# Issuing the first 1 MB load of a matmul kernel as two transfers, of 16 and of 112 partitions

## The chip, the cores and the metric

The kernel runs on one core of one Trainium2 chip. The metric is the device time of one execution in microseconds (us). Every run quoted is fast: none is over 1.5% above the fastest of the same kernel. Differences here are below 1.3%, so every comparison is made with runs of the kernel before taken on the same chip in the same rounds.

The span of a profile (first to last instruction) is about 1.8 us shorter than the device time of the same run: 209.0 us against 210.74 us for the kernel before.

## The reference

```python
batch, m, k, n = 16, 512, 1024, 768          # x: 16 x 512 x 1024, weight: 1024 x 768, float32
def reference(x, weight, bias, residual):
    return (np.matmul(x, weight) + bias + residual).astype(np.float32)
```

Read as 2-D, x has 8192 rows, which are 64 tiles of 128. The kernel reads x (33.6 MB), the residual (25.2 MB) and the weights (3.1 MB), and writes 25.2 MB: 87 MB through the DMA engines.

## The kernel before

Each tile of x is cast to bf16 (`cast`), transposed on TensorE (`transp`), multiplied by the weights into PSUM, the memory that TensorE writes (`mms`), and given bias and residual (`finish`, `pool_add`). Loads go to SBUF, the on-chip memory of 128 rows, called partitions. All transfers except the bias row are issued by SP, in this order:

```python
x_d = x2d.rearrange("(S p j) k -> S p j k", p=P, j=J)      # P = 128 partitions, J = 8 tiles a group

def load_x(S, j0=0, j1=J):
    if S < n_s:
        if j0 == 0:
            x_sb[S] = ring(sb, "x_tile", S, X_BUFS, [P, J, K], FP32)
        K_(nc.sync.dma_start(out=x_sb[S][:, j0:j1, :], in_=x_d[S, :, j0:j1, :]))
...
load_x(0, 0, 2)          # the first load: two tiles, 8 KB a partition, 1 MB
load_x(0, 2, 3)
load_w(0); load_w(1); load_w(2); load_w(3)      # 768 KB each
load_x(0, 3, 4)
load_x(0, 4, 6)
load_x(0, 6, 8)
load_res(0, 0, 4)
load_x(1, 0, 4)
...
keep_warm(12)            # 12 matmuls on zeros, until the first tile is there
cast(0, "dve")
cast(1)
transp(0)
transp(1)
keep_warm(3)
...                      # tile 2, bias, casts of the weights; then the main matmuls
```

## Time and profile before

| what | kernel before | where it is read |
|---|---|---|
| device time, first three runs | 210.83 us (210.65 to 210.95) | times |
| TensorE (PE) busy | 200.4 us of 209.0 | page, part 1 |
| DMA | 98 to 100% busy, about 430 GB/s in the middle | stages |
| first two tiles landed | 5.40 us | start of the casts |
| first main matmul | 9.54 us | timeline |
| last eviction ends, span ends | 203.5 us, 209.0 us | timeline, page |

From the page of the kernel before: the busy times, the row of DMA busy tenths in 40 slices of the span, the bytes, and the chain that ended last.

```profile
PE 200.4 (96%) x1274; PEld 130.6 (63%) x1299; DVE 105.0 (50%) x139; ACT 67.6 (32%) x68; POOL 115.5 (55%) x71
...
DMA  6999999999999999999999999999999999999994
...
DMA packets 5632, 87.23 MB, mean 417 GB/s; under 512 B 625, under 2 KB 753, under 8 KB 1906
...
PE 96%; issue 1%; DVE 1%
```

Two resources look full: PE at 96%, and the DMA row, nearly all nines. The next view shows stages (start and end in us, length, busy us of each engine with instruction counts, granted TensorE clock, DMA share, GB/s).

```profile
20.00:60.00 40.00, 39.69 (x259) 26.37 (x264) 20.82 (x27) 15.19 (x17) 26.78 (x15) 1.00 1.01 428
...
204.00:209.00 5.00, 0.00 (x0) 0.00 (x0) 0.00 (x0) 0.00 (x0) 0.00 (x0) 0.87 0.40 156
```

In the middle both are full. In the last 5 us no compute engine does anything, while the DMA engines still move 156 GB/s on average. The last pieces of the chain of waits show that it stops before that (start, length, what):

```profile
199.15 3.91 PE po L104 x24
203.06 0.02 issue
203.08 0.42 DVE ro L131
```

The chain ends at 203.5 us, and the span at 209.0: the last 5.5 us, the draining of the stores, are in no line of it.

The start, from the timeline (start, busy us, engine, line, operation, count, in brackets the idle time before it and what ended it):

```profile
0.74 0.85 SPq L66 DMA_DIRECT2D x_tile<-in_x_dram  x2
1.19 5.26 PE L170 MATMUL po<-warm 128*128 128x512 bf16 x12 [1.19 <-DVE warm L156]
5.40 0.69 DVE L87 CAST xb<-x_tile 128x1024 bf16<-128x1024 f32 x1 [4.13 <-DMA x_tile<-in_x_dram]
6.28 1.04 PE L95 MATMUL pt<-ident,xb 128*128 128x128 f32 x8
7.16 0.81 PE L170 MATMUL po<-warm 128*128 128x512 bf16 x3
8.54 0.83 ACT L176 CAST w_sb<-ro 128x768 bf16<-128x768 f32 x1 [0.84 <-DMA ro<-in_weight_dram]
9.54 7.31 PE L104 MATMUL po<-w_sb,xt 128*128 128x512 bf16 x43
```

SP issues the first load at 0.74 us; the casts start when it has landed, at 5.40; the first weight slice lands at 8.54.

The DMA engines in the first 8 us, in 40 slices of 0.2 us (busy tenths, then GB/s):

```profile
DMA  0000000087945699897997959999999999999899
GB/s 0 0 0 0 0 0 0 0 164 164 328 123 164 287 492 451 369 492 328 492 410 328 573 205 389 384 430 451 410 492 389 430 430 492 399 399 461 369 430 461
```

Nothing moves before about 1.7 us, and the rate is low for the first microsecond.

### The profile page before, as it was taken

The page shows a single profiled execution, that of the slowest core. Times are in us where ns is not written, and L with a number is a line of the kernel's source. Part 1 is how long each engine was busy: PE and PEld are TensorE (multiplying, and loading weights), DVE is VectorE, ACT ScalarE, POOL GpSimd, SP SyncE. Part 2 cuts the span into 40 slices and gives each one's busy share as a digit, 9 for nine tenths or more (in the row PEclk, how much of TensorE's full clock was granted, in tenths as well). Part 3 has the DMA queues.
Part 4 walks back from the last instruction along what each step waited for, and adds up shares of the span by engine and source line. Part 5 has one row for each costly group of instructions (what it writes and reads, how often), then busy time and mean ns, then how long its engine had stood idle before and what let it go on. Part 6 is the DMA issues. An engine that isn't in the chain of part 4 may idle for free.

```text
span 209.0 us, 3151 instructions
## 1 busy us (share of the span) xinstructions
PE 200.4 (96%) x1274; PEld 130.6 (63%) x1299; DVE 105.0 (50%) x139; ACT 67.6 (32%) x68; POOL 115.5 (55%) x71
## 2 busy tenths in 40 slices
PE   7999999999999999999999999999999999999980
PEld 2566666666666666666666666666666666666650
DVE  0737465445445544554554455455445544545550
ACT  2544315511723062422443054230724233430000
POOL 2000197819965565999189802994069910799000
PEclk9999999999999999999999999999999999999998
DMA  6999999999999999999999999999999999999994
GB/s 239 427 421 431 436 413 440 442 405 436 423 470 422 419 428 398 459 420 436 433 400 472 416 427 447 412 439 412 437 445 414 445 419 427 442 419 428 426 404 168
DMA packets 5632, 87.23 MB, mean 417 GB/s; under 512 B 625, under 2 KB 753, under 8 KB 1906
## 3 DMA queue, kind: packets, MB, share of 16 engines
q1 hardware_dynamic: 5616, 87.03, 97.9%
q8 instruction: 10, 0.16, 0.3%
q14 instruction: 4, 0.03, 0.0%
q10 hardware_dynamic: 2, 0.00, 0.0%
HBM read 61.87 MB, written 25.17 MB: 416 GB/s over the span
## 4 chain that ended last, share of the span: by engine, by line
PE 96%; issue 1%; DVE 1%
PE po L104 79%; PE pt L95 13%; PE po L170 3%; PE po L190 1%; DVE xt L99 0%; DVE ro L131 0%; DVE warm L156 0%
## 5 line engine op out<-in xcount | busy, mean ns | idle before, releaser
L104 PE MATMUL po<-w_sb,xt 128*128 128x512 bf16 (+1 forms) x999 | 175.4, 324 | 1.4
L104 PEld LDWEIGHTS <-xt 128*128 128x128 bf16 x1024 | 100.1, 98 | 59.5 <-DVE xt L99 0.5
L87 ACT CAST xb<-x_tile 128x1024 bf16<-128x1024 f32 x62 | 62.8, 1044 | 114.5 <-DMA x_tile<-in_x_dram 56.9
L121 POOL TENSOR_TENSOR ro<-ro,bias_sb 128x768 f32<-128x768 f32 x40 | 71.2, 1816 | 36.2 <-DMA ro<-in_residual_dram 26.2
L99 DVE COPY xt<-pt 128x512 f32<-128x512 f32 x64 | 44.2, 691 | 86.7 <-PE pt L95 86.5
L121 POOL TENSOR_TENSOR ro<-ro,tmp 128x768 f32<-128x768 f32 x24 | 43.1, 1814 | 41.0 <-DMA ro<-in_residual_dram 30.2
L131 DVE TENSOR_TENSOR ro<-po,ro 128x768 f32<-128x768 f32 (+2 forms) x41 | 38.0, 930 | 2.9 <-PE po L104 2.8
L95 PE MATMUL pt<-ident,xb 128*128 128x128 f32 x256 | 38.2, 273 | 0.0
L95 PEld LDWEIGHTS pt<-ident,xb 128*128 128x128 f32 x256 | 29.8, 141 | 8.1 <-issue 0.6
L129 DVE TENSOR_TENSOR tmp<-po,bias_sb 128x768 f32<-128x768 f32 x24 | 22.8, 949 | 0.6 <-POOL ro L121 0.5
L170 PE MATMUL po<-warm 128*128 128x512 bf16 x15 | 6.1, 579 | 1.2 <-DVE warm L156 1.2
L176 ACT CAST w_sb<-ro 128x768 bf16<-128x768 f32 x4 | 3.3, 832 | 4.0 <-DMA ro<-in_weight_dram 4.0
L170 PEld LDWEIGHTS <-warm 128*128 128x128 bf16 x15 | 1.9, 135 | 4.1 <-issue 2.8
L87 DVE CAST xb<-x_tile 128x1024 bf16<-128x1024 f32 x2 | 1.4, 696 | 4.8 <-DMA x_tile<-in_x_dram 4.8
L178 DVE CAST w_sb<-ro 128x768 bf16<-128x768 f32 x4 | 2.2, 555 | 2.5 <-DMA ro<-in_weight_dram 2.5
L161 ACT ACT_TABLE_LOAD x1 | 1.3, 1283 | 2.0 <-POOL ident masks.py:199 2.0
L190 PE MATMUL po<-tmp 128*128 128x512 f32 (+1 forms) x4 | 1.5, 486 | 0.0
L198 DVE COPY bias_sb<-po 128x768 f32<-128x768 f32 x1 | 1.0, 958 | 0.1
L190 PEld LDWEIGHTS po<-tmp 128*128 128x128 f32 x4 | 0.7, 190 | 0.5 <-issue 0.5
L135 POOL MEMSET tmp<- 128x768 f32 x1 | 0.7, 737 | 0.3 <-POOLq L268 0.3
L156 DVE MEMSET warm<- 128x256 uint32 x1 | 0.3, 272 | 0.9 <-PEq L268 0.9
masks.py:199 POOL TENSOR_SCALAR_AFFINE_SELECT ident<-ident 128x128 f32<-128x128 f32 x1 | 0.3, 292 | 0.1
(8 smaller groups left out, 1.0 us busy)
## 6 DMA issues: line engine op xcount, KB each, us to landing
ro<-in_residual_dram SPq DMA_DIRECT2D x7, 3072.0 KB, 18.1
out_dram<-ro SPq DMA_DIRECT2D x7, 3072.0 KB, 23.9
x_tile<-in_x_dram SPq DMA_DIRECT2D x5, 4096.0 KB, 30.8
x_tile<-in_x_dram SPq DMA_DIRECT2D x4, 2048.0 KB, 27.6
x_tile<-in_x_dram SPq DMA_DIRECT2D x3, 1024.0 KB, 8.6
ro<-in_weight_dram SPq DMA_DIRECT2D x4, 768.0 KB, 9.0
ro<-in_residual_dram SPq DMA_DIRECT2D x2, 1536.0 KB, 21.1
out_dram<-ro SPq DMA_DIRECT2D x1, 1536.0 KB, 11.9
```

The lines of the kernel that those rows point to most:

```text
L87: K_(copy(out=xb[t], in_=x_sb[t // J][:, t % J, :]))
L95: K_(nc.tensor.transpose(out=pt[:, c, :], in_=pairs[:, c * P:(c + 1) * P], identity=ident))
L99: K_(nc.vector.tensor_copy(out=xt[t], in_=pt))
L104: K_(nc.tensor.matmul(po[t][:, n0:n0 + nl], lhsT=both[:, e, :], rhs=w_sb[:, c, e, n0:n0 + nl], start=(i == 0), stop=(i == len(steps) - 1),))
L121: K_(nc.gpsimd.tensor_add(out=r, in0=r, in1=tmp[t] if t < EARLY else bias_sb))
L129: K_(nc.vector.tensor_add(out=tmp[t], in0=p, in1=bias_sb))
L131: K_(nc.vector.tensor_add(out=row(t, n0, nl), in0=p, in1=row(t, n0, nl)))
L161: K_(nc.scalar.copy(out=warm_a, in_=warm_a))
L170: K_(nc.tensor.matmul(warm_ps[:, 0:512], lhsT=warm[:, 0:P], rhs=warm, start=True, stop=True))
L176: K_(nc.scalar.copy(out=w_sb[:, c, e, :], in_=w_st[:, c, e, :]))
L178: K_(nc.vector.tensor_copy(out=w_sb[:, c, e, :], in_=w_st[:, c, e, :]))
L190: K_(nc.tensor.matmul(bias_ps[:, n0:n0 + nl], lhsT=ones, rhs=bias_row[:, n0:n0 + nl], start=True, stop=True,))
```

## The change

The intent appears to be that a small first transfer gets all DMA engines going sooner. The two transfers together move the same 1 MB into the same places.

```diff
-    def load_x(S, j0=0, j1=J):
+    def load_x(S, j0=0, j1=J, p0=0, p1=P):
         if S < n_s:
-            if j0 == 0:
+            if j0 == 0 and p0 == 0:
                 x_sb[S] = ring(sb, "x_tile", S, X_BUFS, [P, J, K], FP32)
-            K_(nc.sync.dma_start(out=x_sb[S][:, j0:j1, :], in_=x_d[S, :, j0:j1, :]))
+            K_(nc.sync.dma_start(
+                out=x_sb[S][p0:p1, j0:j1, :], in_=x_d[S, p0:p1, j0:j1, :]
+            ))
...
-    load_x(0, 0, 2)
+    load_x(0, 0, 2, 0, 16)
+    load_x(0, 0, 2, 16, P)
```

## The prediction

> **What bounds the kernel now.** TensorE. The page gives PE 200.4 us busy of 209.0 (96%), and the chain that ended last is 96% PE; in the stage view PE is busy 39.7 of 40 us in the middle. The DMA engines are close behind (98-100% busy, 417 GB/s). Since PE hardly pauses after 9.5 us (longest wait 0.5 us, for DVE), a delay of the first main matmul moves the end by the same amount.
>
> **What the change does.** One 1 MB load (128 partitions x 8 KB) becomes 128 KB (partitions 0-15) plus 896 KB (16-127). Bytes, compute and the other engines' order stay. SP has 39 rows instead of 38, and its later waits on "eight DMAs ago" move by one place: the load of tile 3 now waits for the bias load, perhaps 2 us past its 3.7 us issue, but its bytes are queued behind 3 MB of weights anyway.
> - Added on SP: one issue, about 0.43 us (two take 0.85 us). Issues run ahead of the data, so it is free, except that the second transfer's descriptors come 0.43 us after the first's.
> - The intent must be an earlier start. In the DMA view of the first 4 us, the issue is at 0.74 us, first packets at 1.7, full rate (430 GB/s) from about 2.75; only about 210 KB move between 1.7 and 2.7 us. An earlier start could win some 0.3 us at most.
> - Against it: the Trainium skill, page "SBUF — State Buffer", section "Door 1: The DMA port swizzle", puts partitions 0-15 on 4 of 16 SBUF ports and gives 104 GB/s measured there. By that page 128 KB takes (estimate) 1.26 us, which holds each of the 16 engines on its single 8 KB row; before, a first packet takes 0.3-1.0 us (mean about 0.65), a later one 0.31. Then 7 rows per engine follow, 2.2 us, on partition groups not aligned with ports. No run here has shown the port effect yet.
> Net estimate: 1.26 - 0.65 = +0.6 us, less a possible 0.1-0.2 us earlier start: both tiles land at about 5.8 us instead of 5.4.
>
> **How much is critical.** Casts start on landing (5.40 us), the first transposes at 6.2 us. Warm-up weight loads are 0.43 us apart and the transposes' come 0.63 us after the last of them, so they already wait for the cast. Tile 2 (landing 6.65 us, transposes 7.75), bias matmuls (8.24), first weight slice (landing 8.5, first main matmul 9.54) are in the same DMA stream, so all move by the stream's delay. From then on PE and stream move together. About 0.3-0.4 us reaches the end.
>
> **Prediction.** 211.15 us, range 210.6 to 211.7. Faster by over 2%: 0.5%; within 2%: 99%; slower: 0.5%. Direction: slower by 0.1-0.6 us 60%, no visible change 25%, faster by 0.1-0.4 us 15%.
>
> **What the profile would show.**
> - Right: first packets still at 1.6-1.7 us; from 1.8 to 2.9 us a rate near 100-150 GB/s; first tiles landing at 5.6-6.1 us, tile 2 and the first weight slice 0.2-0.6 us later, first main matmul at 9.8-10.0 us, PE busy unchanged, total later by the same.
> - Wrong: first packets at 1.3-1.5 us, first tiles before 5.4 us, first main matmul before 9.5 us.
>
> **What would make it wrong.** (1) Buffering hides the port conflict and the smaller transfer starts sooner: up to 0.4 us faster. (2) The 112 partitions spread unevenly, slowing more than estimated. (3) The wait near 18 us absorbs the delay: no change.

## The result, and the profile after

The changed kernel takes 212.25 us (median of 6, 212.13 to 212.57), the kernel before 210.85 us (median of 6, 210.58 to 211.35) on the same chip. The ratio is 1.0067, with a 95% interval of 1.0053 to 1.0081. Here and below a ratio is the mean time of one kernel's fast runs over that of the other's fast runs of the same rounds, so it is not quite the ratio of the medians. The change costs 0.67%, about 1.4 us: inside the 2% band, but above the predicted 211.15 us and outside the range of 210.6 to 211.7.

The page of the changed kernel, the lines that answer to those of before:

```profile
PE 201.7 (96%) x1274; PEld 131.8 (63%) x1299; DVE 104.9 (50%) x139; ACT 68.3 (32%) x68; POOL 115.7 (55%) x71
...
DMA  6999999999999999999999999999999999999984
...
PE 93%; DMA 3%; DVE 1%; issue 1%; SPq 0%; DVEq 0%
```

The averages hardly move. The chain gained a DMA piece at its start. The timeline of the start shows more:

```profile
0.74 1.32 SPq L66 DMA_DIRECT2D x_tile<-in_x_dram  x3
7.41 0.69 DVE L89 CAST xb<-x_tile 128x1024 bf16<-128x1024 f32 x1 [6.13 <-DMA x_tile<-in_x_dram]
8.25 1.68 PE L97 MATMUL pt<-ident,xb 128*128 128x128 f32 x8 [2.37 <-DVE xb L89]
9.72 1.49 PE L173 MATMUL po<-warm 128*128 128x512 bf16 x3
10.41 0.83 ACT L179 CAST w_sb<-ro 128x768 bf16<-128x768 f32 x1 [0.83 <-DMA ro<-in_weight_dram]
13.20 7.31 PE L106 MATMUL po<-w_sb,xt 128*128 128x512 bf16 x43
```

Three things happened.

- The first two tiles land at 7.39 us instead of 5.40, 2.0 us late.
- The whole DMA stream behind them is late: the first weight slice lands at 10.41 instead of 8.54, 1.9 us late.
- TensorE, idle for 2.4 us, comes back slow: the eight transposes take 1.68 us instead of 1.04, the three warm-up matmuls 1.49 instead of 0.81. The first main matmul is 3.66 us late.

The Trainium skill, page "TensorE: Matmul & The Clock Gate", section "Part 1: The HAM clock gate", says that the array runs at half speed until about 3.4 us of sustained work. This trace agrees: after the pause the same instructions take 1.6 to 1.8 times as long, with a mean granted clock of 0.64 from 8 to 10 us, 0.51 from 10 to 12, and 1.00 from 12 on. In the traces the granted clock fell to 0.5 after every early pause of TensorE of 2.0 to 3.6 us (the change, e6, e7, e8, e10, e12), and not after those of 0.5 to 1.1 us (e3, e4, e11).

The DMA engines in the first 8 us, after:

```profile
DMA  0000000059399207497989769898889996899999
GB/s 0 0 0 0 0 0 0 0 123 369 164 328 205 41 0 246 164 492 287 410 246 410 179 164 369 246 410 246 225 225 266 205 266 184 328 451 369 492 461 420
```

The first packets do not come earlier (1.75 us in both traces), and from 3 to 6.6 us the engines are busy but move only 281 GB/s on average, against 414 before. The packet records, of which the views print only sums, give the same in another form: of the 128 packets of 8 KB that make up the load, 19 took over 350 ns before and 108 do now; packets 17 to 128, all of the 112-partition transfer, take 490 ns on average instead of 319. The first 16, the small transfer, take 455 ns, less than the 654 ns of the first 16 before, and have all ended at 2.40 us. So by these records it is the packets of the large transfer that are slow, not those of the small one. Whether the first 14 of the large one (756 to 1146 ns) wait for the small one cannot be told. The stage from 3 to 6 us, after the change:

```profile
3.00:6.00 3.00, 2.88 (x9) 0.88 (x7) 0.00 (x0) 0.50 (x2) 0.00 (x0) 1.00 0.96 288
```

At the end, the last pieces of the chain after the change:

```profile
202.81 3.92 PE po L106 x24
206.72 0.02 issue
206.75 0.42 DVE ro L133
```

TensorE is still 3.66 us late (206.72 against 203.06), but the span grew by only 1.8 us in these two profiles and the time by 1.4 us. A delay of TensorE by 3.66 us therefore did not reach the end as such. Either some of it vanished in slack and the rest counts, or only the DMA stream counts, whose delay (1.5 to 1.9 us) is about the size of the loss. To have one figure for the stream I use the time at which its first 40 MB had ended, from the packet records: 96.78 us before, 98.41 after, 1.63 us later.

### The profile page after: what moved, and what is told of

Read it like the earlier page. It is cut to its first block, busy times and chain, and to the rows that moved or that the text cites. A ratio compares the mean times of both kernels' runs of the same rounds, so it can differ in the third digit from the quotient of the medians.

```text
span 210.8 us, 3154 instructions
## 1 busy us (share of the span) xinstructions
PE 201.7 (96%) x1274; PEld 131.8 (63%) x1299; DVE 104.9 (50%) x139; ACT 68.3 (32%) x68; POOL 115.7 (55%) x71
## 4 chain that ended last, share of the span: by engine, by line
PE 93%; DMA 3%; DVE 1%; issue 1%; SPq 0%; DVEq 0%
PE po L106 78%; PE pt L97 14%; DMA x_tile<-in_x_dram 3%; PE po L193 1%; PE po L173 1%; DVE xb L89 0%; DVE xt L101 0%; DVE ro L133 0%; SPq L66 0%; DVEq L89 0%
## 5 line engine op out<-in xcount | busy, mean ns | idle before, releaser
L89 ACT CAST xb<-x_tile 128x1024 bf16<-128x1024 f32 x62 | 63.5, 1045 | 117.5 <-PE pt L97 67.1
L97 PE MATMUL pt<-ident,xb 128*128 128x128 f32 x256 | 39.3, 278 | 2.4 <-DVE xb L89 2.4
L97 PEld LDWEIGHTS pt<-ident,xb 128*128 128x128 f32 x256 | 30.8, 144 | 10.5 <-issue 3.3
```

What stands on the lines that cost most here:

```text
L89: K_(copy(out=xb[t], in_=x_sb[t // J][:, t % J, :]))
L97: K_(nc.tensor.transpose(out=pt[:, c, :], in_=pairs[:, c * P:(c + 1) * P], identity=ident))
```

## The experiments

There were two questions: which of the two delays makes the loss, and why the split load is slow.

The table gathers the runs. "10 MB" is the time at which the first 10 MB of the stream had ended in the trace, less that of before (26.46 us); "loss" is the ratio less one, times 211 us.

| run | edit | 10 MB, us later | ratio (95% interval) | loss, us |
|---|---|---|---|---|
| the change | 16 + 112 | 1.54 | 1.0067 (1.0053 to 1.0081) | 1.4 |
| e1 | before, TensorE 2.0 us late | 0.00 | 0.9992 (0.9976 to 1.0009) | -0.2 |
| e2 | before, 17 warm-ups | 0.04 | 0.9988 (0.9971 to 1.0005) | -0.3 |
| e3 | changed, TensorE kept warm | 1.47 | 1.0051 (1.0034 to 1.0068) | 1.1 |
| e4 | 16 + 112 on a later load | 1.82 | 1.0069 (1.0052 to 1.0086) | 1.5 |
| e5 | cut by tile, 128 + 128 partitions | 0.20 | 0.9997 (0.9984 to 1.0011) | -0.1 |
| e6 | 64 + 64 | 2.65 | 1.0124 (1.0108 to 1.0139) | 2.6 |
| e7 | 112 + 16 | 1.57 | 1.0095 (1.0079 to 1.0110) | 2.0 |
| e8 | 96 + 32 | 1.88 | 1.0068 (1.0054 to 1.0081) | 1.4 |
| e9 | before, TensorE 3.6 us late | 0.02 | 1.0001 (0.9979 to 1.0023) | 0.0 |
| e10 | 64 + 64, other addresses read | 2.43 | 1.0108 (1.0091 to 1.0125) | 2.3 |
| e11 | whole, other addresses read | 0.19 | 0.9999 (0.9984 to 1.0015) | 0.0 |
| e12 | even + odd partitions | 1.01 | 1.0041 (1.0017 to 1.0065) | 0.9 |

The median of the kernel before was 210.85 us on the chip of the first comparison, 211.23 us beside e1 to e4, 211.19 beside e5 to e8 and 211.35 beside e9 to e12, so ratios are compared, not times.

### e1, e2 and e9: the kernel before, with TensorE alone made late

```diff
-    keep_warm(12)
+    keep_warm(21)        # e1;  e2: 17;  e9: 29
```

> The kernel before with 21 instead of 12 warm-up matmuls: TensorE starts its transposes about 3.5 us later (9 x 0.43, less what it waits today), at full clock, and no DMA changes. Theory 1 (after the change the end is set by the late TensorE, and the kernel before has some 2 us of slack between the last matmul and the end of its DMA stream): first main matmul near 13.0 us instead of 9.54, total up by 1.2 to 1.8 us, the same as the change. Theory 2 (both kernels end with their DMA stream, which the change delays by 1.9 us): total within 0.3 us of before. Theory 3, that of the prediction (TensorE alone sets the end): up by 3.5 us.

> The kernel before with 17 warm-up matmuls: TensorE about 1.8 us late, DMA unchanged. Theories 1 and 2: within the slack, total up by 0 to 0.4 us. Theory 3: up by 1.8 us.

> The kernel before with 29 warm-up matmuls: TensorE late by about 3.7 us (the lateness of the changed kernel), DMA stream as before. By the traces the last store could start 2.0 us later before TensorE catches up with the stream: before, its DMA work ends 3.9 us after the last store is issued, in the changed kernel 1.95 us after. So a total up by 1.3 to 1.8 us if that slack is 2.0 us, which would mean that in the changed kernel TensorE and the stream end together; a total up by less than 0.5 us if the slack is larger and the stream alone counts.

e2 was a miss as an experiment: in its trace the warm-ups come 0.43 us apart only until about 4.3 us and 0.22 us apart from then on, so 17 of them end when the 12 of before did, which were all slow (5.35 us after their start, against 5.26). The first main matmul stayed at 9.62 us, and the run says nothing. The moment at which the warm-ups become fast differs from trace to trace (about 4.3 us in e2, 6.4 in e1, 6.2 in e9), so how late TensorE was in the executions that were not profiled is not known; at e2's moment e9 would still be some 2.6 us late (estimate: 3.6 us less four to five warm-ups that are 0.21 us shorter).

e1 moved TensorE by 2.0 us (first main matmul 11.55 us) instead of the intended 3.5, since its warm-ups too became fast, at about 6.4 us. The time did not change. e9 moved it by 3.6 us, as much as the change had done. Its timeline:

```profile
1.19 8.86 PE L170 MATMUL po<-warm 128*128 128x512 bf16 x29 [1.19 <-DVE warm L156]
5.34 0.69 DVE L87 CAST xb<-x_tile 128x1024 bf16<-128x1024 f32 x1 [4.07 <-DMA x_tile<-in_x_dram]
8.61 0.83 ACT L176 CAST w_sb<-ro 128x768 bf16<-128x768 f32 x1 [0.84 <-DMA ro<-in_weight_dram]
13.13 3.09 PE L104 MATMUL po<-w_sb,xt 128*128 128x512 bf16 x17
```

The loads land as before, and the first main matmul is at 13.13 us. The last pieces of its chain of waits:

```profile
204.96 1.70 PE po L104 x11
206.66 0.02 issue
206.68 0.42 DVE ro L131
```

TensorE is still 3.6 us late at the end (206.66 against 203.06), yet the time is that of before: 211.33 us beside 211.35, ratio 1.0001. The time from the last eviction to the end of the span shrank from 5.5 to 2.8 us (span 209.9 in this profile). So a late TensorE of this size costs nothing that these runs can show (the interval allows 0.5 us). Of the two outcomes expected for e9, the one with 2.0 us of slack is refuted; the slack is at least about 3 us, if the other executions were as late as the profiled one. In the kernel before the DMA stream ends last, not TensorE, and the chain of waits, which was 96% PE, did not show it.

### e3: the changed kernel, with TensorE kept busy

```diff
     # in the changed kernel
-    keep_warm(12)
+    keep_warm(17)
```

> The changed kernel with 17 warm-up matmuls, so that TensorE is busy until the late tiles land and keeps its clock; the DMA stream stays 1.9 us late. Expected in the trace: granted clock back to 1.0 before 20 us, first main matmul near 11.6 us instead of 13.2. Theory 1 (late TensorE sets the end): total falls by 1.0 to 1.5 us, to about 211.0. Theory 2 (late DMA stream sets the end): total stays within 0.3 us of 212.25.

The first main matmul came at 11.04 us instead of 13.20, and the last eviction started at 203.82 us instead of 205.94, so TensorE regained 2.1 us. The loss stayed: ratio 1.0051, where theory 1 needed about 1.000. The median is 212.32 us beside 212.25 for the changed kernel. (Those two were not run on the same chip, but the interval of e3 against its own kernel before excludes theory 1.) The slow clock after the pause is real and costs nothing that these runs can show. The executions of the changed kernel say the same: the one with the highest mean clock (0.996) took 212.18 us, the one with the lowest (0.988) 212.28.

### e4: the same split, on a later load

```diff
-    load_x(0, 0, 2, 0, 16)
-    load_x(0, 0, 2, 16, P)
+    load_x(0, 0, 2)
...
-    load_x(0, 6, 8)
+    load_x(0, 6, 8, 0, 16)
+    load_x(0, 6, 8, 16, P)
```

> The first load whole, and instead the load of tiles 6 and 7 (also 1 MB, 9th in the stream, needed late) split into 16 and 112 partitions. The same DMA shapes, but nothing that TensorE waits for early. If the shape costs DMA time in mid-stream too, packets of 8 KB in that stretch take 400 to 550 ns instead of 309, and all later loads land 0.8 to 1.6 us later. Theory 2 then expects a total up by 0.8 to 1.6 us; theory 1 a total up by at most 0.4 us, since TensorE does not start late. If the cost is that of the cold start alone, no later landing moves and the total is as before.

The start is as before (first tiles at 5.36 us, first main matmul at 9.49). The stretch of the split load, first before, then e4, in the view of stages (the last columns are clock, DMA share, GB/s):

```profile
15.00:18.00 3.00, 2.94 (x20) 1.76 (x18) 2.33 (x4) 0.03 (x1) 0.00 (x0) 1.00 1.01 421
18.00:21.00 3.00, 2.87 (x18) 1.92 (x20) 1.86 (x4) 2.47 (x3) 0.00 (x0) 1.00 1.01 423
21.00:24.00 3.00, 3.00 (x21) 2.00 (x20) 1.52 (x3) 1.51 (x2) 0.00 (x0) 1.00 1.04 433
```

```profile
15.00:18.00 3.00, 2.89 (x20) 1.71 (x18) 2.37 (x4) 0.00 (x0) 0.00 (x0) 1.00 1.10 371
18.00:21.00 3.00, 2.69 (x17) 1.65 (x18) 1.36 (x2) 1.99 (x2) 0.00 (x0) 1.00 0.96 259
21.00:24.00 3.00, 3.00 (x22) 1.97 (x21) 1.52 (x3) 1.52 (x2) 0.00 (x0) 1.00 1.03 388
```

The DMA engines are as busy, but the rate falls from 423 to 259 GB/s. The bytes missing in these 9 us are (50 + 164 + 45) GB/s x 3 us = 0.78 MB, which at 428 GB/s are 1.8 us; that is the lag that the packet records show (1.82 us at 10 MB). The packets of 8 KB that start from 18 to 21 us take 484 ns on average instead of 314, as expected (400 to 550). The loss is 1.5 us, that of the change itself. So the cost is not one of the cold start and not one of waiting for the first tile: it is DMA time spent on this shape, at the start of the stream or in its middle, and it goes to the end nearly undiminished.

### e5: two transfers, but cut by tile

```diff
-    load_x(0, 0, 2)
+    load_x(0, 0, 1)
+    load_x(0, 1, 2)
```

> The first load again as two transfers, but cut by tile: all 128 partitions each time, 4 KB a partition. Same extra issue, same doubled start, no uneven partitions. Port theory (time is lost because each engine's run of partitions is not aligned with the SBUF ports): both tiles land within 0.2 us of 5.40 us, later loads unmoved, total as before. Splitting theory (a second transfer costs a second start of the engines, whatever its shape): landing near 6 to 7 us and a total up by about 1 us or more.

Tile 0 landed at 4.38 us and tile 1 at 5.63 us, near the 5.40 of before. In this trace the next two loads landed about 1.1 us late (tile 2 at 7.75, first weight slice at 9.61), with a few single packets of 480 to 900 ns around 5 us. I do not know why, and the stream had caught up to 0.20 us by 10 MB. The expectation of later loads unmoved failed in this trace, and the first main matmul came at 10.64 us, 1.1 us late. The time did not change. An extra transfer in front, with its issue and its second start, is therefore free when it spans all partitions; the splitting theory is refuted.

### e6, e7 and e8: other cuts by partition

```diff
-    load_x(0, 0, 2, 0, 16)
-    load_x(0, 0, 2, 16, P)
+    load_x(0, 0, 2, 0, 64)      # e6;   e7: 0, 112;   e8: 0, 96
+    load_x(0, 0, 2, 64, P)      # e6;   e7: 112, P;   e8: 96, P
```

> Cut into partitions 0-63 and 64-127: each half reaches 8 of 16 ports by the Trainium skill. A small model of mine (16 engines, equal consecutive runs of partitions, each port and engine 8 KB per 309 ns as measured) gives 2.48 us more than one whole transfer: landing near 7.9 us, stream late by 2.5 us, total up by 2 to 2.5 us. Splitting theory: the same as the change, total up by 1.4 us.

> 112 partitions first, then 16. The same model gives 1.24 us more than whole (the change itself: 1.55 us): landing near 6.6 us, total up by 0.9 to 1.3 us. If the loss were that of starting with a tiny transfer, it would vanish here: landing within 0.3 us of before.

> 96 partitions first (6 an engine), then 32 (2 an engine). The model gives 1.24 us more than whole, as for 112 + 16: landing near 6.6 us, total up by 0.9 to 1.3 us. If only the odd 7 rows an engine hurt, and not the ports, this lands within 0.3 us of before.

The small model of these expectations takes the port map of the Trainium skill, page "SBUF — State Buffer", section "Door 1: The DMA port swizzle", lets each engine take an equal, consecutive run of the transfer's partitions, and gives each engine and each port 8 KB per 309 ns, the duration of an undisturbed packet in the trace. That engines take consecutive runs is my assumption; the trace does not name engines or ports. The model's working is not on record, it was made after the change had been measured, and taken at its word it does not fit the whole load: with runs of 8 partitions, the engine that has 0-7 and the one that has 32-39 would share two ports by the same map and have to take turns, while the trace shows no such delay (319 ns a packet). Read it as a rough guide.

| cut | model, us more than whole | stream lag, us | loss, us |
|---|---|---|---|
| 16 + 112 (the change) | 1.55 | 1.54 | 1.4 |
| 64 + 64 (e6) | 2.48 | 2.65 | 2.6 |
| 112 + 16 (e7) | 1.24 | 1.57 | 2.0 |
| 96 + 32 (e8) | 1.24 | 1.88 | 1.4 |

All cuts by partition cost, and 64 + 64 costs most, as the model says; its figure for e7 is 0.3 us too low and for e8 0.6, and it has the lag of the change above theirs, where it is the smallest. In e6 the 1 MB takes 5.1 us from the first packet to the end of the last (2.08 to 7.19 us), 205 GB/s; the page gives 196 GB/s, measured with 1 MiB, for partitions 0-63. Both expectations of e7 and e8 that would have cleared the ports (no loss when the large piece goes first; no loss when each engine has an even number of rows) failed. The landing times, 7.39 and 7.43 us, were also later than the 6.6 us expected. e7 scattered more than the others (212.57 to 213.26 us), and its profiled run was its fastest, so its lag of 1.57 us belongs to a run that lost 1.4 us (212.57 against 211.19).

### e10 and e11: the same destinations, other addresses read

```diff
     # in place of the two load_x(0, 0, 2, ...) of the change
+    dense = x2d[0:2 * P, :].rearrange("(p j) k -> p j k", j=2)     # one dense 1 MB block
+    for p0, p1 in [(0, 64), (64, P)]:                               # e11: [(0, P)]
+        K_(nc.sync.dma_start(out=x_sb[0][p0:p1, 0:2, :], in_=dense[p0:p1, :, :]))
```

> As the cut into 64 and 64 partitions, but the two tiles are read from one dense 1 MB block (8 KB pitch instead of 32 KB): a wrong result on purpose, the same SBUF side. Write-side theory (SBUF ports): still up by 2.2 to 2.8 us. Read-side theory (the pattern of HBM addresses slows the halves): the loss changes clearly, by more than 0.7 us.

> The first load whole, 128 partitions, from the same dense block (wrong result on purpose): the control of the run above. Write-side theory: as before within 0.3 us. Read-side theory: changed by as much as the halves change.

Both give a wrong result. The halves lose 1.08% as against 1.24%, and the whole load loses nothing. Stage views from 3 to 6 us, e10 and then e11:

```profile
3.00:6.00 3.00, 3.00 (x9) 0.93 (x7) 0.60 (x1) 1.10 (x3) 0.00 (x0) 1.00 1.00 413
```

```profile
3.00:6.00 3.00, 3.00 (x9) 0.93 (x7) 0.00 (x0) 0.48 (x2) 0.00 (x0) 1.00 1.05 222
```

```profile
3.00:6.00 3.00, 2.59 (x9) 0.77 (x7) 0.33 (x1) 0.82 (x3) 0.00 (x0) 1.00 0.98 407
```

The first fence is the kernel before (413 GB/s), the second e10 (222), the third e11 (407). The pitch of the addresses read does not matter. Nor are fewer packets under way at a time: in e10 their times still fill 16 engines (DMA share 1.05) while the rate is 222 GB/s. What is left of the causes considered is how the transfer is cut by partitions.

### e12: even and odd partitions

```diff
     # in place of the two load_x(0, 0, 2, ...) of the change
+    for q in range(2):
+        K_(nc.sync.dma_start(out=x_sb[0][q::2, 0:2, :], in_=x_d[0, q::2, 0:2, :]))
```

> Cut into the 64 even and the 64 odd partitions. Each transfer now touches all 16 ports. If what counts is how many ports a transfer reaches, no loss: total as before. If what counts is which ports the 16 engines hit at the same time, and each engine takes consecutive rows of the transfer, two engines share a port at every step, as for 64 + 64: up by 2.2 to 2.8 us, or less if the engines drift apart. Read side here: every other 32 KB row, another pattern than in 64 + 64.

The loss is 0.41%, about 0.9 us (0.4 to 1.4), between the two expectations: not zero, although each transfer touches all 16 ports by the skill's table, and well under the 2.5 us of 64 + 64. Packets 17 to 128 take 352 ns on average, between 319 (whole) and 560 (64 + 64). This fits engines that meet on a port at first and then drift apart, but that part is argued, not shown.

## Why the prediction was wrong

**"What bounds the kernel now. TensorE."** Wrong. TensorE is as good as always busy, but delaying it by 3.6 us (e9) left the time unchanged, while 1.5 to 2.7 us of lag in the DMA stream (the change, e4, e6) reached the end almost in full. The DMA stream is the chain that ends last. The reading failed where the chain of waits was taken as complete: it ends at 203.5 us, and 5.5 us of draining stores follow. The Trainium skill, page "Perfetto Trace Analysis", section "Identifying the Most-Contended Engine", warns that busy time of matmuls is a poor measure of how close TensorE is to its limit; that is a warning about TensorE alone, and the failure here was another: the 96% was true, and yet it was not TensorE that ended last.

**"A delay of the first main matmul moves the end by the same amount."** Wrong: 3.66 us late after the change, 1.4 us of loss, and none in e9.

**"Net estimate: 1.26 - 0.65 = +0.6 us": the cost of the split.** The delay was forecast for the wrong transfer. The 16 partitions at 104 GB/s, 1.26 us, did not show: by the packet records this transfer took 0.65 us (1.75 to 2.40 us, 202 GB/s), with 455 ns a packet where the first 16 of before took 654. The term that failed in size is "7 rows per engine follow, 2.2 us": these packets took 490 ns on average, so 7 rows take 3.4 us, 1.2 us more than counted. I had seen that the groups of 7 are not aligned with ports and left it as a risk. Taken per engine, 0.46 + 3.43 us against 0.65 + 7 x 0.319 before is 1.0 us of the 1.54 us of lag; the rest is not assigned. That the sign came out right is in part luck, since the forecast +0.6 came from the transfer whose own packets were not slow. The first tiles landed at 7.39 us, not 5.8, and the stream lagged by 1.5 to 1.9 us, not 0.4.

**"From then on PE and stream move together. About 0.3-0.4 us reaches the end."** Wrong: TensorE fell 3.66 us behind, the stream about 1.6 us. TensorE's part beyond that is the slow clock after a pause that the prediction did not foresee: kept warm (e3), it was 1.5 us late. They moved apart, and the end followed the stream: 1.4 us of its lag of about 1.5 to 1.6 us arrived there, not 0.3 to 0.4.

**What held.** The direction; the first packets at 1.75 us, no earlier than before; that the extra issue is free (e5); that bytes and instruction order elsewhere stay. The predicted 100-150 GB/s between 1.8 and 2.9 us did not show: the rate there was 201, and the loss came from 3 to 6.6 us (281 against 414), in the transfer of 112. "PE busy unchanged" missed by 1.3 us (201.7 against 200.4), the slow clock.

**What stays open.** That the lost time depends on how the partitions are cut is shown (e5, e6, e12), and that the pitch of the addresses read does not cause it (e10, e11). That it arises on the destination side follows only by elimination: no run changed the destination with the same addresses read. That it is the 16 SBUF ports rests on the skill's map and on a model that comes within 0.2 us for the change and e6 but not for e7 and e8, has no figure for e12, and does not fit the whole load. None of these runs gives a version that beats the kernel before: e1, e2, e5 and e9 are level with it.

## What to carry to other kernels

When a kernel keeps both TensorE and the DMA engines full, find which ends last before costing a change: look at what still moves after the last instruction of the chain, and make one of the two late on purpose, which takes a one-line edit. Keep large loads spanning all 128 partitions, even when only a small first piece is wanted; if such a piece is needed, cut along the free dimension (within each partition), which cost no time here (though in its trace the next two loads landed 1.1 us late), while every cut along partitions cost 0.9 to 2.6 us for 1 MB. The cost was the same at the start of the saturated DMA stream and in its middle (e4), so moving it off the start did not help.

## What the Trainium skill lacked or had wrong

- "DMA: Bandwidth & Descriptors", "Rules for kernel authors", says of two transfers to disjoint partition halves not to bother, since they share the same engines either way. It does not say there how much slower they are, though the 196 GB/s of the SBUF page, quoted at e6, lets one expect it: 64 + 64 cost 2.6 us for 1 MB (ratio 1.0124).
- "SBUF — State Buffer", "Door 1", counts the ports that a transfer's partitions reach. That is not enough: even and odd partitions reach all 16 by its table and still lost 0.41%; partitions 16 to 127 reach all 16 too and lost time (490 ns a packet instead of 319).
- "DMA: Bandwidth & Descriptors" has the number of engines for a transfer and the layout over engines and ports for 128 partitions; for fewer, no page that I read says which partitions each engine takes when SP issues the load. A model with consecutive runs gave 1.55, 2.48, 1.24 and 1.24 us where the stream lagged by 1.54, 2.65, 1.57 and 1.88 us.
- No page that I read gives the slow start of idle DMA engines: the first 16 packets of 8 KB took 654 ns on average, the other 112 of that load 319 ns.
- "Perfetto Trace Analysis" does not advise comparing the end of the compute with the end of the span; here those 5.5 us decided what bound the kernel.
